# Weight sums made in DRAM: eleven of sixteen pairs of the joint down projection by seven products

## The chip, the cores and the metric

The kernel runs on one core of a Trainium2 chip. The metric is the device time of one execution in microseconds (us). The core has a matrix engine (PE, with its weight loads counted apart as PEld), a vector engine (DVE), a scalar engine (ACT) and GpSimd (POOL). SyncE (SP) issues most of the DMAs and POOL the others. A matmul takes a stationary operand from SBUF (128x128), streams a moving one (up to 512 columns) and adds into a bank of PSUM.

## The reference, cut to what matters

One block of a diffusion transformer with 256 tokens, 256 context tokens, a model width of 2048 and a feed-forward width of 5632, all in float32: adaptive layer norm, a projection to recurrent, attention and gate parts, a gated merge, and a convolutional feed-forward part. The change is in the last matmul of

```python
def conv_ffn(h, w_up, conv_w, conv_b, w_down):
    a, u = jnp.split(h @ w_up, 2, axis=-1)
    return (jax.nn.silu(depthwise_conv(a, conv_w, conv_b)) * u) @ w_down
...
        new_x = x_mid + mod_x[:, 5][:, None, :] * ffn_x
```

`w_down` is 5632 x 2048. Each column of `ffn_x` is scaled by a gate and added to `x_mid`.

## The kernel before, in words

**Precision.** Every float32 operand is split in two parts: `hi`, a cast by ACT, and `lo`, the rest, a subtraction by DVE. A product of two such operands is three matmuls (`mm3`): hi by hi, hi by lo and lo by hi. Below, "group" means such a three.

**The weight stream.** All weights lie in DRAM in one array `wst`, in rows of [128, 1024] floats (512 KB), in the order of use; SP fetches them. `Stream.load` and `chunk` do the same steps: load into a tile `raw` (five buffers), cast into `whi`, subtract into `wlo` (three buffers each). `chunk` keeps its casts and subtractions in the order of its calls. It can use a tile of its own instead: the tag `araw` has two buffers, which the `ada` loads use as well.

**Stages.** In order of time: norm statistics and the first adaptive parameters (0 to 150 us), the projections with the recurrent part and attention (to about 650 us), the gated merge (to about 790 us), the output projection (to about 917 us), the up projection in three groups of 16, 16 and 12 tiles of 128 feed-forward columns, and the down projection. After the first two up groups (about 917 to 1291 us) comes the joint stage, `down_two`: the down projection of their 32 tiles (1291 to 1456 us). Then come the third up group and its own down projection.

**The joint stage.** It has two halves, one for each 1024 output columns. A half walks 16 pairs of tiles. A pair is a product of 2x2 blocks: two token blocks by two feed-forward tiles, times two feed-forward tiles by two column blocks of 512. The function `half` makes it in one of two ways:

- A *plain* pair loads two rows (first `rb` with w21 and w22, then `ra` with w11 and w12) and makes eight groups, 24 matmuls.
- A *seven-product* pair (those in `SEVEN`) makes seven groups, 21 matmuls, from sums of blocks. The sums of activations (`s1`, `s2`, `s4`) are made by `seven_acts` when the up projection has made the two tiles. The four sums of weights, t1 to t4, are made by DVE within `half`: four adds of 128x512 in `four`, from `ra` and `rb` into two `araw` tiles, which are then split.

The splits of a seven-product pair are those of `rb` (two blocks), of w11 (one block, into a tile of its own, `wone`), of t1 and t3, and of t2 and t4. The groups follow in this order: two with w21 and w22, one with w11, two with t1 and t3, two with t2 and t4. The accumulators of the seven products are put together by `combine` after the last seven-product pair and by four more DVE operations at the half's end.

**Background work.** `ada_steps` makes the remaining adaptive parameters (`ada` below): 128 rows of 512 KB that POOL loads into `araw` and that DVE multiplies and adds into `acc`. The function `ada` advances it. It is called by hand in the early stages, by the stream according to `st.pace` (a call is due after 16/pace loads), and after each tile of the up projection (`up_evac`). `homes` tells in which buffers the loads land. The steps are given a lower priority than the work around them, by `LAG`.

**Residual rows.** `xn` holds the rows of `x_mid`, 2 MB in the tag `qo`, from the output projection to the end.

**Order of the work.** The kernel is written in the tile language. A planner orders each engine's instructions by priority, which is program order shifted by `high_priority`, when the tiles and data that they need are there in its plan. `issue_after` puts instructions behind a given one on the same engine.

Of the kernel before, what the change touches and what calls it, by code (L numbers as in the profile page):

```python
# [1 line left out]

# [5 lines left out]
F32 = mybir.dt.float32  # L8
F32R = mybir.dt.float32r
U32 = mybir.dt.uint32  # L10
AF = mybir.ActivationFunctionType
ALU = mybir.AluOpType
AX = mybir.AxisListType

P = 128
T = 256
D = 2048
KT = D // P
# [14 lines left out]
CONSTS = [("ident", 128), ("ones", 128), ("ropec", 256), ("ropes", 256), ("amask", 256), ("hmask", 256),  # L33
          ("m64", T)]
FF_GROUPS = [(0, 16), (16, 16), (32, 12)]
SEVEN = (1, 3, 5, 7, 9, 11, 13)
GSEVEN = (2, 4, 6)
LATE = (18, 20, 17)
LAST_ORDER = (1, 2, 4, 0, 3, 5)
# [15 lines left out]
def block_kernel(ctx, tc, xct, xr, prm, cst, ada2, wst, out):  # L55
    nc = tc.nc
    V, S, PE = nc.vector, nc.scalar, nc.tensor

    cons = ctx.enter_context(tc.tile_pool(name="cons", bufs=1))
    big = ctx.enter_context(tc.tile_pool(name="big", bufs=1))  # L60
# [5 lines left out]
    dram = ctx.enter_context(tc.tile_pool(name="dram", bufs=1, space=bass.MemoryType.DRAM))  # L66
# [36 lines left out]
    eps_c, one_c = par("eps"), par("one")  # L103
    S.preload_act_table_set("natural_log_exp_and_others")

    class Stream:
# [26 lines left out]
        def next(self, n=1):  # L133
            if self.pos == 8:
                self.load()
            sl = slice(self.pos * P, (self.pos + n) * P)
            self.pos += n
            return self.hi[:, sl], self.lo[:, sl]

    st = Stream()  # L140
# [3 lines left out]
    def chunk(parts, make, tag="raw", home=None):  # L144
        with tc.high_priority(offset=min(LEAD, max(0, tc.tile_snap_priority() - base[0]))), ExitStack() as inorder:
            raw = strm.tile([P, 1024], F32, name=tag, bufs=5 if tag == "raw" else 2) if isinstance(tag, str) else tag
            hi, lo = home or [strm.tile([P, 1024], F32R, name=nm, bufs=3) for nm in ("whi", "wlo")]
            for b in behind:
                inorder.enter_context(tc.issue_after(b.ins))
            make(raw)  # L150
            w = slice(0, 512 * parts)
            a = S.copy(hi[:, w], raw[:, w])  # L152
            b = V.tensor_tensor(lo[:, w], raw[:, w], hi[:, w].bitcast(F32), op=ALU.subtract)  # L153
            behind[:] = [a, b]
        return raw, [(hi[:, 512 * i:512 * i + 512], lo[:, 512 * i:512 * i + 512]) for i in range(parts)]

    def fetch(raw):
        nc.sync.dma_start(raw, wst[st.half])
        st.half += 1

    def split(hi, lo, src):
        S.copy(hi, src)
        V.tensor_tensor(lo, src, hi.bitcast(F32), op=ALU.subtract)

    def combine(sev, y, post):
        S.copy(y[0], sev[0])
        V.tensor_tensor(y[2], sev[2], y[0], op=ALU.subtract)
        V.tensor_tensor(y[1], sev[1], y[2], op=ALU.add)
        V.tensor_tensor(y[2], sev[3], y[2], op=ALU.add)
        V.tensor_tensor(y[3], sev[3], y[1], op=ALU.add)  # L170
        if post:
            for b in range(4):
                post(b)

    def half(act, order, seven, sums, banks, y, own, made={}, post=None, tail=False):

        norm, sev = banks

        def add(b, a, w, start=False, stop=False):
            mm3(b, *a, *w, start, stop)  # L180
        seven = [p for p in order if p in seven]
        plains = [p for p in order if p not in seven]
        for p in order:
            k1, k2 = 2 * p, 2 * p + 1
            rb, (w21, w22) = chunk(2, fetch)
            a11, a21, a12, a22 = act(k1, 0), act(k1, 1), act(k2, 0), act(k2, 1)
            st0, plain = p == order[0], p == plains[0]
            if p not in seven:
                if p == order[-1]:
                    ra, (w11, w12) = chunk(2, fetch)  # L190
                    for b, u1, u2, v1, v2 in ((0, a11, a12, w11, w21), (1, a11, a12, w12, w22), (2, a21, a22, w11, w21),
                                              (3, a21, a22, w12, w22)):
                        for w in [slice(0, 512)] if not tail or b < 3 else [slice(0, 256), slice(256, 512)]:
                            add(norm[b][:, w], u1, [v[:, w] for v in v1])
                            add(norm[b][:, w], u2, [v[:, w] for v in v2], stop=True)
                    break
                add(norm[0], a12, w21, st0)
                add(norm[2], a22, w21, st0)
                add(norm[1], a12, w22, st0)
                add(norm[3], a22, w22, plain)  # L200
                ra, (w11, w12) = chunk(2, fetch)
                add(norm[0], a11, w11)
                add(norm[2], a21, w11)
                add(norm[1], a11, w12)
                add(norm[3], a21, w12)
                continue
            f, l = p == seven[0], p == seven[-1]
            if f:
                sev = sev()
            s1, s2, s4, *s3 = sums[p]  # L210
            add(norm[0], a12, w21, st0)
            add(norm[1], s4, w22, st0)
            ra, (w11,) = chunk(1, fetch, home=own)
            add(sev[0], a11, w11, f, l)
            if p in made:
                t1, t3, t2, t4 = made[p]
                add(sev[1], s1, t1, f, l)
                add(sev[3], s3[0] if s3 else a21, t3, f, l)
                add(sev[2], s2, t2, f, l)
                add(norm[2], a22, t4, st0)  # L220
                if l:
                    combine(sev, y, post)
                continue

            r4 = strm.tile([P, 1024], F32, name="araw", bufs=2)

            def four(raw):
                V.tensor_tensor(raw[:, 0:512], ra[:, 0:512], ra[:, 512:], op=ALU.add)
                V.tensor_tensor(raw[:, 512:], ra[:, 512:], rb[:, 512:], op=ALU.add)  # L229
                V.tensor_tensor(r4[:, 0:512], raw[:, 0:512], rb[:, 512:], op=ALU.add)  # L230
                V.tensor_tensor(r4[:, 512:], r4[:, 0:512], rb[:, 0:512], op=ALU.add)
            r2, (t1, t3) = chunk(2, four, "araw")
            add(sev[1], s1, t1, f, l)
            add(sev[3], s3[0] if s3 else a21, t3, f, l)

            _, (t2, t4) = chunk(2, lambda raw: None, r4)
            add(sev[2], s2, t2, f, l)
            add(norm[2], a22, t4, st0)
            if l:
                combine(sev, y, post)  # L240
        if post:
            return
        with tc.high_priority(offset=RUSH):
            for b in range(4):
                V.tensor_tensor(y[b], norm[b], y[b], op=ALU.subtract if b == 2 else ALU.add)
# [218 lines left out]
    qo = big.tile([P, 2, H, T], F32, name="qo", tag="qo")  # L464
# [9 lines left out]
    homes = [wide]  # L474
# [38 lines left out]
                yield  # L513

    ada_it = ada_steps()

    def ada(n=1):
        with tc.high_priority(offset=-LAG), tc.issue_after(st.last.ins):
            for _ in range(n):
                next(ada_it, None)  # L520

    tasks = []

# [441 lines left out]
    for c in range(4):  # L965
        st.pace = 0
        if c % 2 == 0:
            norm = [bank() for _ in range(4)]
# [91 lines left out]
                norm2(2 * (k - 6))  # L1060


    def fold_pre(dst, o):
        b = smalltile(1)
        S.copy(b, o[:, T:T + 1])
        V.tensor_tensor(dst, o[:, 0:T], ssa[:, T:], op=ALU.mult)  # L1066
        S.activation(dst, dst, AF.Identity, bias=b)
# [31 lines left out]
    def seven_acts(p, gt, i, s1, s2):  # L1099
        if not sums:  # L1100
            sums["b"] = big.tile([P, 2, 2, 3 * P], F32R, name="sb", tag="sb")
        n = (SEVEN + LATE).index(p)
        if n == 2:
            sums["a"] = big.tile([P, 5, 2, 3 * P], F32R, name="sa", tag="v")
        d = sums["b"][:, n % 7] if n % 7 < 2 else spare2 if n > 7 else sums["a"][:, n - 2]
        sums[p] = d
        w = scr.tile([P, 512], F32, name="t")
        V.tensor_tensor(w[:, 0:P], s1[:, P:], s2[:, P:], op=ALU.subtract)
        s3 = w[:, 3 * P:] if p == LATE[-1] else s1[:, P:]
        V.tensor_tensor(s3, s1[:, P:], s1[:, 0:P], op=ALU.subtract)  # L1110
        V.tensor_tensor(w[:, P:2 * P], s1[:, 0:P], w[:, 0:P], op=ALU.subtract)
        V.tensor_tensor(w[:, 2 * P:3 * P], s2[:, 0:P], w[:, P:2 * P], op=ALU.subtract)
        if p == LATE[-1]:
            split(d[:, 0, :], d[:, 1, :], w)
            return
        split(gt[:, i - 1, 1, P:], gt[:, i - 1, 0, P:], s1[:, P:])
        split(d[:, 0, :], d[:, 1, :], w[:, 0:3 * P])
# [76 lines left out]
    up(1, g1)  # L1194
    for _ in ada_it:
        pass
    assert not tasks
    gate = [None, cst_t[:, 2 * P:2 * P + 1024]]
    line = to_line(gate2)
# [2 lines left out]
        get_rows(line, n, gate[n])  # L1202
    get_gate(1)
    y0, y1 = down_two(g0, g1)
    gate[0] = big.tile([P, 1024], F32, name="gate", tag="acc")
    get_gate(0)
    for b in range(4):
# [181 lines left out]
```

## Time and profile before

| | |
|---|---|
| median of three runs | 1658.97 us (1658.14 to 1659.23) |
| profiled execution | 1659.95 us |
| its span, first to last instruction | 1658.2 us |
| PE busy | 1640.0 us, 99% |
| DVE busy | 1303.4 us, 79% |
| ACT busy | 862.2 us, 52% |
| moved by DMA | 377.03 MB, 227 GB/s on average |

The profile is of one execution, and the time outside its span is launch and end. A row of a group gives the line of the kernel, the engine, the operation, the tiles written and read, the count, and then the busy time and the mean duration; behind the second bar stands the idle time of that engine just before these instructions and what ended it. A line such as L73 is that of a helper (all matmuls), so the tiles tell what is meant.

### The profile page before, as it was taken

How to read it: one execution, taken by the hardware profiler on the slowest of the kernel's cores; microseconds unless marked ns; L12 is line 12 of the kernel's file. 1: busy time of each engine (PE TensorE's matmuls, PEld its weight loads, DVE VectorE, ACT ScalarE, POOL GpSimd, SP SyncE). 2: the span in 40 equal slices, each digit the busy share in tenths (PEclk: the TensorE clock that was granted, in tenths of full speed). 3: DMA queues.
4: the chain of work that ended last, by engine and by line, in shares of the span. 5: the costliest groups of instructions: out<-in, count | busy, mean ns of one | idle time of the engine just before them, and what ended most of it. 6: DMA issues, size and time to landing. Idle time of an engine off the chain costs nothing.

```text
span 1658.2 us, 23679 instructions
## 1 busy us (share of the span) xinstructions
PE 1640.0 (99%) x8827; PEld 1356.2 (82%) x8827; DVE 1303.4 (79%) x2001; ACT 862.2 (52%) x1302; POOL 68.8 (4%) x133
## 2 busy tenths in 40 slices
PE   7999999999999999999999999999999999999998
PEld 3668888888888888888888988888888888888887
DVE  3448986675889976888888798878877898998788
ACT  4336553443645664545445665555555555556552
POOL 0000100100000000000011000000000000000000
PEclk9999999999999999999999999999999999999999
DMA  9996834634456665676878577767655566666654
GB/s 379 407 373 242 298 117 153 204 110 151 166 204 206 219 216 174 239 278 213 314 258 312 171 239 263 251 224 267 238 190 189 202 206 201 217 208 223 218 189 165
DMA packets 104260, 377.03 MB, mean 227 GB/s; under 512 B 11696, under 2 KB 12112, under 8 KB 103888
## 3 DMA queue, kind: packets, MB, share of 16 engines
q1 hardware_dynamic: 85568, 307.87, 52.2%
q0 software_dynamic: 18576, 67.64, 12.6%
q8 instruction: 69, 1.13, 0.3%
q14 instruction: 47, 0.39, 0.1%
HBM read 373.36 MB, written 2.11 MB: 226 GB/s over the span
## 4 chain that ended last, share of the span: by engine, by line
PE 87%; DVE 5%; DMA 4%; issue 3%; ACT 1%; SPq 0%; POOL 0%; DVEq 0%; ACTq 0%; POOLq 0%
PE bankm L73 76%; PE banks L73 9%; DMA ringv<-in_wst_dram 1%; DVE wlo L119 1%; DMA ringq<-in_wst_dram 1%; DVE acc L497 1%; DMA ringkT<-in_wst_dram 1%; PE banks L505 0%; PE banks L872 0%; DMA araw<-in_ada_dram 0%; DMA xraw<-in_xct_dram 0%; PE banks L705 0%; PE banks L900 0%; PE banks L697 0%; ACT whi L118 0%
## 5 line engine op out<-in xcount | busy, mean ns | idle before, releaser
L73 PE MATMUL bankm<-hl,whi 128*128 128x512 f32 (+1 forms) x2048 | 626.6, 388 | 0.1
L118 ACT CAST whi<-raw 128x1024 fp32r<-128x1024 f32 (+1 forms) x378 | 394.4, 1045 | 390.4 <-PE bankm L73 339.6
L119 DVE TENSOR_TENSOR wlo<-raw,whi 128x1024 fp32r<-128x1024 f32 (+1 forms) x378 | 459.0, 1216 | 175.6 <-ACT whi L118 174.5
L73 PE MATMUL bankm<-whi,hl 128*128 128x512 f32 x1548 | 498.1, 393 | 1.2 <-ACT hl L340 0.9
L73 PE MATMUL bankm<-hl,wlo 128*128 128x256 f32 (+2 forms) x1760 | 396.0, 293 | 1.3 <-DVE wlo L119 1.3
L73 PEld LDWEIGHTS bankm<-hl,wlo 128*128 128x128 f32 x1760 | 330.5, 188 | 75.9 <-DVE wlo L119 2.2
L73 PEld LDWEIGHTS bankm<-hl,whi 128*128 128x128 f32 x2048 | 327.6, 189 | 17.6 <-DVE fs L1066 0.4
L73 PEld LDWEIGHTS bankm<-whi,hl 128*128 128x128 f32 x1548 | 289.6, 188 | 63.2 <-ACT hl L340 2.6
L73 PE MATMUL bankm<-wlo,hl 128*128 128x512 f32 x774 | 301.6, 390 | 0.0
L73 PEld LDWEIGHTS bankm<-wlo,hl 128*128 128x128 f32 x774 | 145.4, 188 | 29.1 <-DVE wlo L119 0.2
L497 DVE SCALAR_TENSOR_TENSOR acc<-araw,csil,acc 128x1024 f32<-128x1024 f32 x120 | 153.2, 1277 | 0.7 <-DMA araw<-in_ada_dram 0.2
L153 DVE TENSOR_TENSOR wlo<-raw,whi 128x1024 fp32r<-128x1024 f32 x95 | 115.7, 1223 | 30.3 <-ACT whi L152 26.7
L152 ACT CAST whi<-raw 128x1024 fp32r<-128x1024 f32 x95 | 99.9, 1054 | 73.3 <-PE bankm L73 53.1
L492 POOL DMA_DIRECT2D araw<-in_ada_dram x128 | 68.1, 532 | 1111.9 <-DVE acc L497 635.3
L73 PE MATMUL bankm<-whi,yb 128*128 128x512 f32 x256 | 82.1, 396 | 0.0
L152 ACT CAST whi<-araw 128x1024 fp32r<-128x1024 f32 x44 | 46.2, 1053 | 62.5 <-DVE araw L229 56.2
L73 PEld LDWEIGHTS bankm<-whi,yb 128*128 128x128 f32 x256 | 47.9, 188 | 10.0
L153 DVE TENSOR_TENSOR wlo<-araw,whi 128x1024 fp32r<-128x1024 f32 x44 | 53.7, 1222 | 1.8 <-ACT whi L152 0.5
L73 PE MATMUL bankm<-wlo,yb 128*128 128x512 f32 x128 | 50.4, 394 | 0.0
L1079 ACT ACTIVATE fs<-fs,prm 128x256 f32<-128x256 f32 x44 | 26.4, 601 | 45.7 <-DVE fs L554 45.7
L73 PE MATMUL bankm<-whi,g 128*128 128x512 f32 x124 | 41.3, 389 | 0.0
L321 DVE TENSOR_REDUCE tn<-banks 128x8 f32<-128x32 f32 (+1 forms) x9 | 1.7, 187 | 45.9 <-ACT whi L118 42.8
(346 smaller groups left out, 1704.0 us busy)
## 6 DMA issues: line engine op xcount, KB each, us to landing
raw<-in_wst_dram SPq DMA_DIRECT2D x495, 512.0 KB, 4.1
araw<-in_ada_dram POOLq DMA_DIRECT2D x128, 512.0 KB, 4.7
ringv<-in_wst_dram SPq DMA_DIRECT2D x24, 512.0 KB, 10.1
ringq<-in_wst_dram SPq DMA_DIRECT2D x20, 512.0 KB, 9.9
araw<-in_wst_dram SPq DMA_DIRECT2D x10, 512.0 KB, 9.9
xraw<-in_xct_dram SPq DMA_DIRECT2D x8, 512.0 KB, 8.3
raw<-in_wst_dram SPq DMA_DIRECT2D x7, 384.0 KB, 9.9
ringkT<-in_wst_dram SPq DMA_DIRECT2D x5, 512.0 KB, 9.9
```

The costliest lines, as they stand in the source:

```text
L73: return PE.matmul(o, l, r, start=start, stop=stop, skip_group_check=True)
L118: S.copy(hi, raw)
L119: self.last = V.tensor_tensor(lo, raw, hi.bitcast(F32), op=ALU.subtract)
L152: a = S.copy(hi[:, w], raw[:, w])
L153: b = V.tensor_tensor(lo[:, w], raw[:, w], hi[:, w].bitcast(F32), op=ALU.subtract)
L321: V.tensor_reduce(m8, aps[:, 0:w].rearrange("p (q g c) -> p q c g", q=2 * n, g=4)[:, :, 0:2, :], axis=AX.X, op=ALU.add)
L492: nc.gpsimd.dma_start(raw, ada2[idx])
L497: V.scalar_tensor_tensor(acc, raw, csil[:, kt, 0:1], acc, op0=ALU.mult, op1=ALU.add)
L1079: S.activation(t, s, AF.Identity, bias=cb[:, f:f + 1], scale=cw[:, f, 1:2])
```

## The change

- `SEVEN` grows from seven to eleven of the sixteen pairs: 1, 2, 3, 5, 6, 7, 9, 10, 11, 13, 14. Pairs 0, 4, 8, 12 and 15 remain plain.
- For each half and each of these pairs a DRAM tile `d` of [128, 2, 1024] floats is filled by POOL: one copy of the pair's two rows, and four transfers of [128, 512] that add into their destination. At the end it holds t4, t2 and t1, t3. These are 22 copies and 88 adding transfers.
- They are issued by `ada`: two steps per call, or one where `st.pace` is set, and none while `homes` is `apart` or `late`. Ahead of them DVE writes one element (`pins`) and POOL copies it, so that POOL waits for DVE to come to that place.
- In `half` such a pair loads the first half of `ra` only (w11) and takes t1, t3 and t4, t2 by two SP loads into `araw`. The adds by DVE are not used in the joint stage any more.
- The sums of activations of four more pairs need room, and take it in the tag `qo`. `xn` leaves it: it is written to a DRAM tile `kept` by POOL after the norm of the up projection, and read back into a new tile in `qo` after the joint stage in program order.

```diff
-SEVEN = (1, 3, 5, 7, 9, 11, 13)
+SEVEN = (1, 2, 3, 5, 6, 7, 9, 10, 11, 13, 14)
...
+    def fetch_half(raw):
+        nc.sync.dma_start(raw[:, 0:512], wst[st.half, :, 0:512])
+        st.half += 1
+
+    dsums = {}
+    JOINT = wst.shape[0] - 24 - 2 * FF_GROUPS[2][1] * KT // 8 - 64
+
+    def sum_steps(n):
+        ds = []
+        for p in SEVEN:
+            at = JOINT + 32 * n
+            d = dram.tile([P, 2, 1024], F32, name="sum%d" % len(dsums))
+            dsums[at, p] = d
+            ds.append((d, at + 2 * p))
+        for d, r in ds:
+            yield lambda d=d, r=r: nc.gpsimd.dma_start(d, wst[r:r + 2].rearrange("k p c -> p k c"))
+        for d, r in ds:
+            yield lambda d=d, r=r: nc.gpsimd.dma_start(d[:, 1, 0:512], wst[r + 1, :, 512:], accum_op=ALU.add)
+        for d, r in ds:
+            yield lambda d=d, r=r: nc.gpsimd.dma_start(d[:, 1, 512:], wst[r, :, 512:], accum_op=ALU.add)
+        for d, r in ds:
+            yield lambda d=d, r=r: nc.gpsimd.dma_start(d[:, 0, 512:], d[:, 1, 0:512], accum_op=ALU.add)
+        for d, r in ds:
+            yield lambda d=d, r=r: nc.gpsimd.dma_start(d[:, 0, 0:512], d[:, 0, 512:], accum_op=ALU.add)
+
+    sum_it = itertools.chain(sum_steps(0), sum_steps(1))
...
-            ra, (w11,) = chunk(1, fetch, home=own)
+            ra, (w11,) = chunk(1, fetch_half if (at, p) in dsums else fetch, home=own)
...
+            if (at, p) in dsums:
+                d = dsums[at, p]
+                _, (t1, t3) = chunk(2, lambda raw: nc.sync.dma_start(raw, d[:, 1]), "araw")
+                add(sev[1], s1, t1, f, l)
+                add(sev[3], s3[0] if s3 else a21, t3, f, l)
+                _, (t4, t2) = chunk(2, lambda raw: nc.sync.dma_start(raw, d[:, 0]), "araw")
...
             for _ in range(n):
                 next(ada_it, None)
+            fs = list(itertools.islice(sum_it, 0 if homes[0] in (apart, late) else 1 if st.pace else 2))
+            if fs:
+                pin = pins[:, len(pinned) % 40:len(pinned) % 40 + 1]
+                V.tensor_copy(pin, one_c)
+                pinned.append(nc.gpsimd.tensor_copy(pin, pin))
+                with tc.issue_after(pinned[-1].ins):
+                    for f in fs:
+                        f()
...
+    kept = dram.tile([P, 2, 2, 1024], F32, name="kept")
+    nc.gpsimd.dma_start(kept, xn)
...
+        if n == 2:
+            sums["c"] = big.tile([P, 5, 2, 3 * P], F32R, name="sc", tag="qo")
+        if n == 6:
             sums["a"] = big.tile([P, 5, 2, 3 * P], F32R, name="sa", tag="v")
...
     y0, y1 = down_two(g0, g1)
+    xn = big.tile([P, 2, 2, 1024], F32, name="xn", tag="qo")
+    nc.gpsimd.dma_start(xn, kept)
```

More of the change, by code (lines that the diff above doesn't have):

```diff
@@ L1 @@
+import itertools
 from contextlib import ExitStack
@@ L177, in half @@
         norm, sev = banks
+        at = st.half
         def add(b, a, w, start=False, stop=False):
@@ L218, in half @@
                 add(sev[3], s3[0] if s3 else a21, t3, f, l)
+                add(sev[2], s2, t2, f, l)
+                add(norm[2], a22, t4, st0)
+                if l:
+                    combine(sev, y, post)
+                continue
+            if (at, p) in dsums:
[4 more added lines that the diff above has]
+                _, (t4, t2) = chunk(2, lambda raw: nc.sync.dma_start(raw, d[:, 0]), "araw")
                 add(sev[2], s2, t2, f, l)
@@ L515, in block_kernel @@
     ada_it = ada_steps()
+    pins = cons.tile([P, 40], F32, name="pins")
+    pinned = []
     def ada(n=1):
@@ L1102, in seven_acts @@
         n = (SEVEN + LATE).index(p)
+        m = len(SEVEN)
         if n == 2:
+            sums["c"] = big.tile([P, 5, 2, 3 * P], F32R, name="sc", tag="qo")
+        if n == 6:
             sums["a"] = big.tile([P, 5, 2, 3 * P], F32R, name="sa", tag="v")
-        d = sums["b"][:, n % 7] if n % 7 < 2 else spare2 if n > 7 else sums["a"][:, n - 2]
+        d = sums["b"][:, n % m] if n % m < 2 else spare2 if n > m else sums["c"][:, n - 2] if n < 6 else sums["a"][:, n - 6]
         sums[p] = d
@@ L1196, in block_kernel @@
         pass
+    assert next(sum_it, None) is None
     assert not tasks
```

## The prediction

> **What bounds the kernel now.** I began with the page: busy time, slices, queues.
>
> ```profile
> span 1658.2 us, 23679 instructions
> PE 1640.0 (99%) x8827; PEld 1356.2 (82%) x8827; DVE 1303.4 (79%) x2001; ACT 862.2 (52%) x1302; POOL 68.8 (4%) x133
> PEclk9999999999999999999999999999999999999999
> q1 hardware_dynamic: 85568, 307.87, 52.2%
> q0 software_dynamic: 18576, 67.64, 12.6%
> ```
>
> PE is never short of clock and is busy 99% of the span, so a change pays only through fewer products, or costs through new waits of PE. The joint stage (first matmul at 1291 us, last at 1456) and the stages that get new work I then read in the table of windows.
>
> ```profile
> 150.00:206.00 56.00, 54.72 (x358) 46.66 (x357) 55.02 (x89) 32.79 (x57) 8.46 (x16) 1.00 0.81 285
> 206.00:290.00 84.00, 83.75 (x596) 70.13 (x595) 63.29 (x144) 36.49 (x76) 4.19 (x8) 1.00 0.41 138
> 290.00:446.00 156.00, 156.00 (x914) 129.71 (x913) 108.48 (x215) 69.22 (x130) 9.58 (x19) 1.00 0.45 152
> 446.00:490.00 44.00, 43.43 (x270) 35.40 (x269) 38.80 (x76) 23.30 (x44) 3.18 (x6) 1.00 0.59 205
> 490.00:650.00 160.00, 159.95 (x753) 131.31 (x752) 130.08 (x226) 90.66 (x142) 8.47 (x16) 1.00 0.63 211
> 956.00:1291.00 335.00, 335.00 (x1931) 292.40 (x1930) 264.41 (x389) 188.46 (x294) 14.82 (x28) 1.00 0.67 232
> 1291.00:1374.00 83.00, 82.75 (x365) 67.58 (x364) 73.67 (x86) 45.77 (x52) 0.00 (x0) 1.00 0.61 209
> 1374.00:1456.00 82.00, 82.00 (x364) 67.83 (x363) 74.84 (x86) 44.98 (x47) 0.00 (x0) 1.00 0.64 209
> ```
>
> The columns are busy PE, weight loads, DVE, ACT and POOL, then clock, DMA share and GB/s. In both halves of the joint stage PE idles 0.25 us in 165; DVE is at 90%, the DMA engines at 61 to 64%. One window is different: from 150 to 206 us DVE is full (55.02 of 56) and the DMA share is 0.81. The chain of waits gives the pace of a plain pair and a seven-product pair of the joint stage:
>
> ```profile
> 1322.36 8.16 PE bankm L73 x36
> 1330.52 2.04 PE banks L73 x9
> ```
>
> 45 products take 10.20 us, 0.2267 us each. A plain pair (24) takes 5.44 us, a seven-product pair (21) takes 4.76.
>
> **The change, part by part.**
>
> *Removed products.* Four more pairs in each half, 8 in all, lose 3 products each: 24 x 0.2267 = **-5.4 us**, all of it on the path, since PE does not wait. This is the whole prize, 0.33%.
>
> *Removed sums on DVE.* 14 pairs (before) lose four adds of 128x512 each:
>
> ```profile
> L228 DVE TENSOR_TENSOR araw<-raw 128x512 f32<-128x512 f32 x13 | 8.9, 685 | 0.0
> L153 DVE TENSOR_TENSOR wlo<-araw,whi 128x1024 fp32r<-128x1024 f32 x27 | 33.0, 1222 | 0.8
> L152 ACT CAST whi<-raw 128x1024 fp32r<-128x1024 f32 x45 | 47.3, 1054 | 25.1 <-PE bankm L73 16.4 <-PE banks L73 8.7
> ```
>
> That is 56 x 0.685 = 38 us of DVE, hidden behind PE before, so worth nothing by itself.
>
> *New loads in the joint stage.* A seven-product pair now loads 0.524 MB (second row) + 0.262 (half of the first) + 2 x 0.524 (the sums) = 1.835 MB; it loaded 1.049. Over 22 such pairs and 10 plain ones that is 50.9 MB; at PE's pace (726 - 24 products, 159 us) it is 320 GB/s, and by the window rows (0.61 at 209 GB/s) a share of 0.93. It still fits; the point is the buffers. Both sums go to tile "araw", which has two buffers, one for each sum of a pair. So a sum's buffer must be loaded, cast by ACT, subtracted by DVE and freed once per pair. The hops, from the timeline:
>
> ```profile
> 1328.44 2.51 DVE L153 TENSOR_TENSOR wlo<-araw,whi 128x1024 fp32r<-128x1024 f32 x2
> 1331.01 1.23 DVE L153 TENSOR_TENSOR wlo<-raw,whi 128x1024 fp32r<-128x1024 f32 x1
> 1331.92 1.05 ACT L152 CAST whi<-raw 128x1024 fp32r<-128x1024 f32 x1 [0.94 <-PE banks L73]
> 1332.26 6.82 SPq L158 DMA_DIRECT2D raw<-in_wst_dram  x4
> 1333.00 2.59 DVE L153 TENSOR_TENSOR wlo<-raw,whi 128x1024 fp32r<-128x1024 f32 x2 [0.77 <-ACT whi L152]
> ```
>
> DVE ends at 1332.24 and SP issues at 1332.26; ACT ends at 1332.97 and DVE starts at 1333.00. With 0.03 from landing to ACT, the circle is L + 0.03 + 1.05 + 0.03 + 1.22 + 0.02 = L + 2.35 us, L being the time from issue to landing of 512 KB. It has to be no longer than 4.76 us, so L no longer than 2.41. The first line below is that of "raw" from 1300 to 1445 us, the second that of 750 to 900 us, where 282 GB/s moved:
>
> ```profile
> DMA to landing us min/median/max: 3.0/3.5/5.7
> raw<-in_wst_dram SPq DMA_DIRECT2D x54, 512.0 KB, 4.8
> ```
>
> No landing there is as short as 2.41. At 320 GB/s I take **3.65 us**: the joint stage's own row, raised a little, since a sum's load is issued when its buffer frees and not from a long queue. Bounds 3.0 and 4.8. So each seven-product pair that follows another one comes 6.00 - 4.76 = 1.24 us late, against what the first of a group has in hand. That is: the split tiles whi and wlo have three buffers and a seven-product pair uses all three, so the split of its last sum cannot begin before the plain pair ahead of it is done; it takes 0.03 + 1.05 + 0.03 + 1.22 = 2.33 us, and PE needs it after five groups of three products and one product, 3.63 us: 1.30 us in hand. The groups are (1,2,3), (5,6,7), (9,10,11), (13,14). A group of three stalls 2 x 1.24 - 1.30 = 1.18 us, a group of two not at all (0.06 left). Pair 15 is last and plain, and each of its groups needs its second row: two splits behind that of pair 14 (2.51 us, the first of these lines) against 1.13 us of products left and 0.23: 1.15 - 0.06 = 1.1 us. One half: 3 x 1.18 + 1.1 = 4.6; both: **+9.3 us**. At L = 3.0 it is 0.9, at 3.5 it is 7.2, at 4.8 (1.09 for the group of two, too) it is 25.
>
> By the Trainium skill ("DMA: Bandwidth & Descriptors", section "Anatomy of one DMA — SWDGE (gpsimd) path") a transfer costs about 2.0 us and its bytes at 436 GB/s, an estimate of 3.2 us for 512 KB; the stalls would be 3.4 us and the sum 1662. The row's median, 3.5, is longer at two thirds of the traffic, so I stay with the row.
>
> *Making the sums.* 22 copies of 1.049 MB and 88 adding transfers of 0.262 MB go through POOL's queue, 2 steps per `ada` call (1 where `st.pace` is set). Counting the calls: 30 before the attention part (60 steps), 30 up to 650 us (30 steps), none while homes are `apart` or `late`, the last 20 after 956 us. No row shows a DRAM-to-DRAM copy or an add. The nearest is the same queue from 150 to 206 us, and the issues there:
>
> ```profile
> q0 software_dynamic: 2144, 7.83, 41.8%
> araw<-in_ada_dram POOLq DMA_DIRECT2D x16, 512.0 KB, 4.8
> DVE acc L495 <- DMA araw<-in_ada_dram: 2.7, 1, 2.7
> ```
>
> 0.418 x 56 us for 7.83 MB is 2.99 us of all 16 engines per MB: 69 us for the copies and 69 for the adds, twice that if an add counts both things it reads. From 150 to 650 us fall 122 to 176 of these; the windows have 223 free (the sum of each one's length by one minus its share). Overall it fits; between 150 and 206 it does not. 16 `ada` loads mean about 10 calls, so 11 copies and 9 adds, 41 us or more where 11 are free. They spill to 206 to 290, where 50 are free, but `ada` loads stand behind them in POOL's queue, and `acc` on a full DVE waits for those; splits and PE stand behind `acc`. Bounds: 0 (`acc` is simply done later) and 30 us (all that spills is on the path). I take 2.5, near the lower end, because the ordering is free to put `acc` later and because the copies need not be done early. The 70 pins are tiny DVE copies; the nearest op is
>
> ```profile
> L508 DVE TENSOR_TENSOR modv<-modv,prm 128x8 f32<-128x8 f32 x2 | 0.3, 155 | 0.0
> ```
>
> 0.155 us: 10 in the full window, 1.5 us; elsewhere DVE has room. POOL's wait on a pin holds up only POOL's later loads and sums. Together **+4 us**.
>
> *More activation sums.* Four pairs more go through `seven_acts` in the up stage:
>
> ```profile
> L1108 DVE TENSOR_TENSOR t<-fs 128x128 f32<-128x128 f32 x4 | 1.1, 284 | 0.0
> L163 DVE TENSOR_TENSOR sa<-t,sa 128x384 fp32r<-128x384 f32 x4 | 2.2, 556 | 1.1 <-ACT sa L162 1.1
> ```
>
> 4 x 0.285 + 0.556 + about 0.14 for one split cut in two: 1.84 us a pair, 7.4 in all, in a window with 71 us of free DVE and PE at 335.00 of 335. **0**; without that cover 7.4.
>
> *Rows parked.* xn goes out (2.1 MB, 6.3 us at 2.99) with 0.33 of 335 us of DMA free: 0. It comes back through POOL when the sums in "qo" are last used, pair 7 of the second half, beside loads at a share of 0.93. Bounds 0 and 6.3; I take **+1**, since eight pairs (some 40 us) remain before it is needed and the plain ones have spare DMA.
>
> **Sum.** -5.4 + 9.3 + 4 + 1 = +8.9 on the profiled execution's 1659.95 (1.75 of it outside the span): 1668.8. That execution lies 0.98 above the median, so **1668** against 1658.97.
>
> **Rivals.**
>
> *The circle does not bind* (faster). If the loads land in 3.0, the shortest row, and the sums cost nothing: 0.9 - 5.4 = -4.5, **1654.4**. For it: the two loads of a pair are only two in a short queue. Against: the median is 3.5 at less traffic. From L = 3.3 upward it is no longer faster by a measurable amount. Chance 0.27.
>
> *Between the two*: L near 3.4 and sums for 0 to 2 us: 1656 to 1662. Chance 0.14.
>
> *DMA latency under load.* L = 4.8: -5.4 + 25 + 4 + 1 = +25, **1683**. For it: the row of 750 to 900 us, at less traffic than 320 GB/s. Against: there POOL loaded too, and SP fetched far ahead. Chance 0.14. The Trainium skill says in the same page ("Latency and other measured facts") that an HBM access takes 0.2 us on average and 2 us at high load; the two rows, 3.5 and 4.8, point the same way.
>
> *Making the sums hits the path.* `acc` waits behind copies from 150 to 206: half of the 30 us in place of 4: **1679**. For it: the one row in which DVE already waited for an `ada` load. Against: DVE would have to keep its order. Chance 0.12.
>
> That the sums aren't used is excluded: both sides take the row number from the same count.
>
> **How the numbers follow.** The forecast itself, 1662 to 1674, has 0.33. My bound for a change is 0.2%, 3.3 us, about what can be told apart here. Faster: 0.26, from the first rival. Same: 0.15. Slower: 0.59. The range for 8 in 10 runs from the first rival, **1654**, to the third, **1684**; the forecast's own is 1662 to 1674.
>
> **What would show it.** Right: PE idle of 8 to 10 us in the joint stage, its ACT casts of "araw" preceded by waits for DMA, most in pairs 3, 7, 11 and 15; SP waiting for DVE's subtract on "araw"; products in the stage down from 726 to 702. Wrong: a joint stage of 160 us; landings at 3.0; PE gaps from 150 to 290 us instead, with DVE waiting for `araw<-in_ada_dram`. Loads at 4.8 or more would make 1668 too low.

## The result, and the profile after

The changed kernel takes **1708.43 us** (median of four, 1705.45 to 1709.03) against 1659.1 beside it: a ratio of **1.0294**, 95% interval 1.0276 to 1.0312. It is slower, as forecast, but by 49 us in place of 9, far outside the range of 1654 to 1684. The profiled execution took 1705.45 us, the shortest of the four; what the others spent besides, no trace shows. The page of the kernel after, busy time, clock and queues:

```profile
span 1703.5 us, 24033 instructions
PE 1655.0 (97%) x8803; PEld 1353.6 (79%) x8803; DVE 1291.5 (76%) x2055; ACT 876.2 (51%) x1326; POOL 194.3 (11%) x315
PEclk9999979999999999999999999999999999999999
q0 software_dynamic: 37520, 117.98, 24.8%
```

The 24 products are gone, yet PE idles 48.5 us where it idled 18.2, and the row of the clock has a dent in one slice (213 to 256 us). Where the 45.3 us of span went is seen from the chains of waits, that is, from the work that ended last, followed back to what released it. First two stretches of the chain of before, then the chain of after, in which the same two stretches (40 and 256 products) come back:

```profile
225.98 9.09 PE bankm L73 x40
...
1246.66 44.60 PE bankm L73 x256
```

```profile
174.25 22.22 DMA sum<-in_wst_dram
196.75 19.81 DMA araw<-in_ada_dram
...
244.25 9.09 PE bankm L74 x40
...
1264.95 44.59 PE bankm L74 x256
```

The offset is 18.27 us by 244 us and still 18.29 at 1265: the whole **early loss** lies before 244 us, and nothing is lost in the thousand microseconds after it. The joint stage then runs from 1309.3 to 1502.3, 193.0 us, where it took 165.9: **+27.0**. What comes behind it takes 201.2 us in both. 18.3 + 27.0 = 45.3.

The windows of after, with the columns of the prediction's table (the short ones show the places where the clock fell):

```profile
150.00:206.00 56.00, 55.47 (x358) 46.36 (x358) 44.42 (x88) 31.62 (x55) 16.87 (x25) 1.00 0.97 378
206.00:290.00 84.00, 70.97 (x504) 57.06 (x504) 67.15 (x149) 32.55 (x68) 28.88 (x43) 0.88 0.91 262
224.00:230.00 6.00, 5.44 (x45) 3.12 (x48) 4.63 (x17) 1.37 (x3) 5.21 (x7) 0.50 1.07 322
232.00:234.00 2.00, 2.00 (x6) 1.61 (x5) 1.52 (x3) 0.28 (x1) 0.53 (x1) 0.50 1.14 207
234.00:236.00 2.00, 2.00 (x10) 1.57 (x10) 1.57 (x5) 0.07 (x1) 0.74 (x1) 0.97 1.12 240
490.00:650.00 160.00, 160.00 (x747) 131.56 (x746) 137.65 (x268) 90.86 (x145) 38.16 (x64) 1.00 0.90 273
956.00:1291.00 335.00, 334.90 (x1970) 294.16 (x1969) 273.12 (x428) 193.59 (x310) 33.80 (x58) 1.00 0.77 253
1309.00:1405.00 96.00, 87.82 (x359) 66.48 (x358) 63.49 (x66) 51.91 (x61) 0.00 (x0) 0.98 0.80 271
1329.00:1333.00 4.00, 3.48 (x9) 2.48 (x9) 3.37 (x3) 2.80 (x3) 0.00 (x0) 0.60 0.60 216
1405.00:1508.00 103.00, 92.84 (x385) 70.74 (x385) 68.50 (x71) 53.34 (x59) 0.53 (x1) 0.97 0.81 276
1469.00:1473.00 4.00, 3.80 (x9) 3.02 (x10) 3.11 (x4) 1.77 (x4) 0.00 (x0) 0.50 0.64 210
```

From 150 to 206 us the DMA engines are full (0.97, before 0.81), and DVE, which was full (55.02 of 56), now waits (44.42). From 490 to 650 they are nearly as full (0.90) and PE loses nothing: here a full DMA was dear only where something near the path waited for a transfer. The timeline shows what did, POOL's issue of an `ada` load, then DVE and PE (in brackets the idle time before, and what ended it):

```profile
196.75 0.53 POOL L533 DMA_DIRECT2D araw<-in_ada_dram  x1 [3.98 <-DMA sum<-in_wst_dram]
...
208.48 1.29 DVE L538 SCALAR_TENSOR_TENSOR acc<-araw,csil,acc 128x1024 f32<-128x1024 f32 x1 [11.60 <-DMA araw<-in_ada_dram]
...
224.56 0.43 PE L74 MATMUL banks<-hb 128*32 128x64 f32 x4 [13.03 <-DVE hb L699]
```

For one `ada` load DVE waits 11.60 us, until 208.48. A later one, on the chain above, is late twice: POOL issues it at 196.75, when the copy issued at 174.25 has landed after 22.22 us, and it then takes 19.81 us to land itself. The recurrent part's operations on `hb` come behind these `acc` operations on DVE, the last at 224.22, and PE stands 13.03 us for them. When it goes on, the granted clock is 0.50 until 234 us, so of these 9.5 us about 4.8 are lost besides. 13.0 + 4.8 = 17.8 of the early loss of 18.3.

In the joint stage, one full turn of an `araw` buffer, from SP's issue to SP's next issue into it:

```profile
1339.20 0.33 SPq L256 DMA_DIRECT2D araw<-sum  x1
...
1344.07 1.05 ACT L153 CAST whi<-araw 128x1024 fp32r<-128x1024 f32 x1 [1.55 <-DMA araw<-sum]
1345.15 1.23 DVE L154 TENSOR_TENSOR wlo<-araw,whi 128x1024 fp32r<-128x1024 f32 x1 [1.29 <-ACT whi L153]
1346.40 0.33 SPq L256 DMA_DIRECT2D araw<-sum  x1
```

7.20 us against the 4.76 that PE needs for a pair: the landing (from issue until the data are there) takes 4.87 of it, the hops 2.33. Over the whole stage the landings of "araw" are

```profile
DMA to landing us min/median/max: 3.5/4.9/9.9
```

and the table of waits of after has both losses (total, times, longest):

```profile
ACT whi L153 <- DMA araw<-sum: 48.0, 26, 4.4
...
DVE acc L538 <- DMA araw<-in_ada_dram: 18.2, 5, 11.6
```

The longest wait of the joint stage stands beside the parked rows. In program order the read stands behind the stage, but POOL issues it while the second half still runs, and a sum's load that SP issues 4.6 us later has the longest landing of the stage, 9.9 us:

```profile
1452.32 0.53 POOL L1264 DMA_DIRECT2D xn<-kept  x1 [247.28 <-ACT whi L153]
...
1456.90 0.33 SPq L256 DMA_DIRECT2D araw<-sum  x1
...
1466.85 1.04 ACT L153 CAST whi<-araw 128x1024 fp32r<-128x1024 f32 x1 [4.40 <-DMA araw<-sum]
...
1467.94 0.79 PE L74 MATMUL bankm<-whi,sa 128*128 128x512 f32 x1 [3.90 <-ACT whi L153]
```

Behind these 3.90 us the clock is half until 1473, some 2.6 us more. The same is seen in the four other kernels in which both sums of a pair share a tag (e1, e6, e7 and e11 below): there, too, the longest wait of PE in the stage, 3.7 to 4.6 us, ends 13 to 16 us behind the read's issue. That the read makes it is inferred; no run takes the read out of these kernels.

### The profile page after: what moved, and what is told of

Read it like the earlier page. It is cut to its first block, busy times and chain, and to the rows that moved or that the text cites. A ratio compares the mean times of both kernels' runs of the same rounds, so it can differ in the third digit from the quotient of the medians.

```text
span 1703.5 us, 24033 instructions
## 1 busy us (share of the span) xinstructions
PE 1655.0 (97%) x8803; PEld 1353.6 (79%) x8803; DVE 1291.5 (76%) x2055; ACT 876.2 (51%) x1326; POOL 194.3 (11%) x315
## 3 DMA queue, kind: packets, MB, share of 16 engines
q0 software_dynamic: 37520, 117.98, 24.8%
## 4 chain that ended last, share of the span: by engine, by line
PE 80%; DMA 10%; DVE 5%; issue 3%; ACT 2%; POOL 0%; SPq 0%; ACTq 0%; DVEq 0%; POOLq 0%
PE bankm L74 71%; PE banks L74 7%; DMA araw<-sum 4%; DMA araw<-in_ada_dram 2%; ACT whi L153 1%; DVE wlo L154 1%; DMA sum<-in_wst_dram 1%; DMA ringv<-in_wst_dram 1%; DMA ringq<-in_wst_dram 1%; DVE wlo L120 1%; DMA ringkT<-in_wst_dram 1%; DVE acc L538 1%; PE banks L923 0%; PE banks L546 0%; PE banks L756 0%
## 5 line engine op out<-in xcount | busy, mean ns | idle before, releaser
L74 PE MATMUL bankm<-whi,hl 128*128 128x512 f32 x1524 | 491.5, 393 | 1.6 <-ACT hl L381 1.0
L74 PEld LDWEIGHTS bankm<-whi,hl 128*128 128x128 f32 x1524 | 285.4, 188 | 63.7 <-ACT hl L381 2.6
L74 PE MATMUL bankm<-wlo,hl 128*128 128x512 f32 x762 | 297.0, 391 | 0.0
L533 POOL DMA_DIRECT2D araw<-in_ada_dram x128 | 77.6, 630 | 818.5 <-DVE acc L538 359.0
L538 DVE SCALAR_TENSOR_TENSOR acc<-araw,csil,acc 128x1024 f32<-128x1024 f32 x120 | 153.2, 1277 | 18.6 <-DMA araw<-in_ada_dram 18.2
L154 DVE TENSOR_TENSOR wlo<-raw,whi 128x1024 fp32r<-128x1024 f32 x87 | 105.5, 1221 | 23.2 <-ACT whi L153 21.0
L153 ACT CAST whi<-raw 128x1024 fp32r<-128x1024 f32 x87 | 90.8, 1052 | 60.4 <-PE bankm L74 46.0
L154 DVE TENSOR_TENSOR wlo<-araw,whi 128x1024 fp32r<-128x1024 f32 x60 | 73.4, 1224 | 58.7 <-ACT whi L153 58.1
L153 ACT CAST whi<-araw 128x1024 fp32r<-128x1024 f32 x60 | 63.1, 1051 | 91.7 <-DMA araw<-sum 48.0
L568 POOL COPY pins<-pins 128x1 f32<-128x1 f32 x70 | 41.8, 598 | 133.0 <-DVE pins L567 132.9
L358 ACT COPY t<-banks 128x512 f32<-128x512 f32 (+1 forms) x9 | 4.9, 541 | 62.6 <-PE banks L74 62.6
```

The source lines that it names most:

```text
L74: return PE.matmul(o, l, r, start=start, stop=stop, skip_group_check=True)
L358: S.copy(rows[:, 0:w], aps[:, 0:w])
L533: nc.gpsimd.dma_start(raw, ada2[idx])
L538: V.scalar_tensor_tensor(acc, raw, csil[:, kt, 0:1], acc, op0=ALU.mult, op1=ALU.add)
L568: pinned.append(nc.gpsimd.tensor_copy(pin, pin))
```

## The experiments

There were rival theories for each loss; the expectations give them. The early loss is what is lost ahead of the joint stage. Early: the copies and adds make `ada` loads late, and DVE and PE with them, or something else does it, such as weights that come late. Where it is the `ada` loads, their order in POOL's queue may be the cause, or the engines being full. Joint: the circle of the two `araw` buffers, whose cure is buffers, or simply too many bytes, whose cure would be none.

One reading in the expectations has to be put right first. Several speak of a wait of about 5 us at the end of the joint stage, which came from taking the next stage's first product as the end. There is no such wait. The timeline of PE in e3_late_and_two_tags:

```profile
1454.44 0.49 PE L74 MATMUL bankm<-hl,whi 128*128 128x512 f32 x1
1454.77 0.39 PE L74 MATMUL bankm<-wlo,g 128*128 128x512 f32 x1
...
1459.35 0.39 PE L74 MATMUL bankm<-hl,whi 128*128 128x512 f32 x1
```

One product of the third up group (`hl,whi`) runs ahead of the last 4.6 us of the joint stage (`g`, pair 15), without idle time. The stage ends at 1459.35. In the table the joint stage is counted to the true end; figures in the expectations that end at the early product are 4.8 to 5.2 us shorter wherever pair 14 is made by seven products, and the 200 us in that of e2 run past the end. Each ratio is to executions of the kernel before taken beside that run, with medians of 1658.6 to 1659.2. The last two columns are of one profiled execution each; that of e8 was the shortest of eleven (1656.79).

| kernel | median, us | ratio (95%) | joint stage starts | joint stage, us |
|---|---|---|---|---|
| before | 1659.1 | | 1291.0 | 165.9 |
| after | 1708.43 | 1.0294 (1.0276 to 1.0312) | 1309.3 | 193.0 |
| e1_late_sums | 1690.17 | 1.0186 (1.0171 to 1.0202) | 1289.3 | 197.8 |
| e2_sums_two_tags | 1682.31 | 1.0144 (1.0127 to 1.0161) | 1311.0 | 168.5 |
| e3_late_and_two_tags | 1664.33 | 1.0037 (1.0024 to 1.0050) | 1290.4 | 169.0 |
| e4_sums_unused | 1679.96 | 1.0121 (1.0106 to 1.0136) | 1309.0 | 167.5 |
| e5_last_pair_earlier | 1662.08 | 1.0016 (1.0007 to 1.0025) | 1289.8 | 168.9 |
| e6_copies_by_act | 1720.86 | 1.0372 (1.0358 to 1.0386) | 1320.8 | 195.6 |
| e7_sums_in_raw_tag | 1674.20 | 1.0088 (1.0074 to 1.0102) | 1288.6 | 182.0 |
| e8_last_pair_earlier_and_rows_in_two | 1659.85 | 1.0004 (0.9995 to 1.0013) | 1289.1 | 164.6 |
| e9_ten_pairs | 1659.57 | 1.0002 (0.9993 to 1.0010) | 1290.7 | 165.1 |
| e10_nine_pairs | 1655.80 | 0.9979 (0.9970 to 0.9988) | 1289.0 | 163.0 |
| e11_sums_first | 1705.24 | 1.0275 (1.0261 to 1.0289) | 1304.3 | 197.2 |

**No sums in the first twelve calls of `ada`.**

```diff
+    calls = [0]
...
+            calls[0] += 1
-            fs = list(itertools.islice(sum_it, 0 if homes[0] in (apart, late) else 1 if st.pace else 2))
+            fs = list(itertools.islice(sum_it, 0 if calls[0] <= 12 or homes[0] in (apart, late) else 1 if st.pace else 2))
```

> The changed kernel, but the first 12 calls of the background step issue no sums, so the first eleven copies fall some 60 us later, where DVE and the DMA engines have room. Theory 1 (the copies stood ahead of the ada loads in POOL's queue while DVE was full, and DVE waited in order): the 18.2 us lost before 300 us are gone, the joint stage stays as it is, 1690 us. Theory 2 (the traffic of the sums costs its time wherever it lies): the loss moves to a later stage and the time stays near 1708.

1690.17, as the first theory said. The early windows of e1:

```profile
150.00:206.00 56.00, 56.00 (x367) 48.16 (x366) 55.10 (x90) 33.34 (x59) 8.11 (x16) 1.00 0.83 292
206.00:290.00 84.00, 83.73 (x596) 70.14 (x595) 63.76 (x148) 36.62 (x76) 13.32 (x24) 1.00 0.64 235
```

PE idles 0.27 us in 140 (1.53 before the change), at full clock, and the joint stage starts 20.0 us earlier than in after. So it is the sums at that place that make the early loss. The joint stage keeps its loss (197.8; its clock is 0.98 and 0.95).

**One of the two sums of a pair in the five buffers of "raw".**

```diff
-                _, (t1, t3) = chunk(2, lambda raw: nc.sync.dma_start(raw, d[:, 1]), "araw")
+                _, (t1, t3) = chunk(2, lambda raw: nc.sync.dma_start(raw, d[:, 1]), "raw")
```

> The changed kernel, but the first of a pair's two sum loads goes to the tag of the weight rows (five buffers) and only the second to araw, so an araw buffer has two pairs' time for its circle instead of one. Same bytes, same splits, same products. Theory 1 (the circle load, cast, subtract, free of about 7.25 us per pair sets the joint stage): the joint stage falls from 200 us to 160 to 166, the total to 1670 to 1677. Theory 2 (the DMA engines or DRAM are the limit: 50.9 MB at the 275 GB/s seen there): no less than 185 us there, total 1693 or more.

1682.31, above the 1670 to 1677 that were expected, and the joint stage is 168.5 us where it was 193.0. The bytes are the same, so it was the circle and not the bytes. Not all came back: 702 products at 0.2267 are 159.1 us, with the 1.3 that the stage of before has over its products 160.4, so 8 us of waits stay.

**Both edits.**

> Both edits together. Theory 1: the two losses are separate and both go: 1652 to 1660, about the kernel before. Theory 2: 1677 or more.

1664.33, above the 1652 to 1660 that were expected. But the gains of e1 and e2 are 18.3 and 26.1, 44.4 together, and both edits give 44.1: the losses are two and independent. The joint windows of e3, then its landings in "araw":

```profile
1290.00:1372.00 82.00, 80.32 (x349) 64.48 (x348) 61.96 (x63) 51.63 (x60) 0.00 (x0) 1.00 0.87 304
1372.00:1454.00 82.00, 78.83 (x340) 62.91 (x338) 60.05 (x59) 50.48 (x55) 0.58 (x1) 1.00 0.91 324
```

```profile
DMA to landing us min/median/max: 4.0/5.9/11.0
```

More moves per microsecond than in after, each load into "araw" lands later (a median of 5.9 for 4.9), and yet PE stalls less: "araw" now takes one load per pair, so its two buffers leave 2 x 4.76 - 2.35 = 7.2 us for a landing where they left 2.41.

**Sums made, and not read.** `sum_steps` keeps the eleven pairs; the joint stage has its seven old pairs with the sums by DVE.

```diff
-SEVEN = (1, 2, 3, 5, 6, 7, 9, 10, 11, 13, 14)
+SUMMED = (1, 2, 3, 5, 6, 7, 9, 10, 11, 13, 14)
+SEVEN = (1, 3, 5, 7, 9, 11, 13)
...
-            if (at, p) in dsums:
+            if False:
```

> All copies, adds and the parked rows are made as in the changed kernel, but the joint stage is that of before (seven pairs, sums by DVE); the sums in DRAM are not read. Theory 1 (two separate losses): only the early one, 1659 + 18 = 1677. If the parked rows or the later adds cost something too, it shows here above 1677; if the early loss needs the new joint stage, 1659.

1679.96, above the first theory's 1677, which left open a price of the rows. The joint stage starts at 1309.0, 18.0 late, and takes 167.5, 1.6 more than before. So making the sums and parking the rows has a price of its own of about 20 us.

**Pair 14 exchanged for pair 12, on top of both edits.**

```diff
-SEVEN = (1, 2, 3, 5, 6, 7, 9, 10, 11, 13, 14)
+SEVEN = (1, 2, 3, 5, 6, 7, 9, 10, 11, 12, 13)
```

> Late sums and two tags as in e3, and the eleventh seven-product pair is 12 instead of 14, so the last one (13) has two plain pairs behind it, as in the kernel before. In e3 PE waits 4.4 us when the up projection begins again after the joint stage. Theory 1 (the accumulators of the seven products are put together only after pair 14, and the next stage wants their banks one pair later): that wait goes, 1659 to 1661. Theory 2 (the wait comes from the parked rows that are read back): it stays, 1664.

1662.08, between the two theories. The joint stage is 168.9 us, e3's is 169.0: the exchange did nothing there in the profiled executions, and the wait that it was to remove did not exist. The medians of e3 and e5, taken at different times, differ by 2.2 us with ranges that overlap (1662.74 to 1667.67, 1658.99 to 1664.46); what makes this difference stays open.

**The copies issued from ACT's queue**, so that POOL's `ada` loads don't stand behind them (the adds stay with POOL).

```diff
-                S.copy(hi, raw)
+                self.cast = S.copy(hi, raw)
...
-            yield lambda d=d, r=r: nc.gpsimd.dma_start(d, wst[r:r + 2].rearrange("k p c -> p k c"))
+            def copy(d=d, r=r):
+                with tc.issue_after(st.cast.ins):
+                    nc.scalar.dma_start(d, wst[r:r + 2].rearrange("k p c -> p k c"))
+            yield copy
```

> The changed kernel, but the 22 copies are issued on ACT's DMA queue behind the cast of the current weight row, not on POOL's; the adds stay on POOL's. Same bytes at about the same time. Theory 1 (ada loads stood behind copies in POOL's own queue): most of the 18 us before 300 us goes, 1690 to 1694. Theory 2 (the sixteen DMA engines are full from 150 to 230 us, whichever queue the copies are in): the loss stays at 12 to 18 us, 1702 to 1708.

1720.86, slower still and above both theories. The table of waits of e6 from 150 to 300 us, then POOL's issues ahead of one load:

```profile
DVE acc L541 <- DMA araw<-in_ada_dram: 19.4, 4, 14.0
...
PE banks L74 <- DVE hb L699: 17.9, 1, 17.9
```

```profile
196.72 1.71 POOL L182 DMA_DIRECT2D sum<-in_wst_dram  x2
...
198.45 1.76 POOL L182 DMA_DIRECT2D sum<-in_wst_dram  x2
199.56 1.76 POOL L536 DMA_DIRECT2D araw<-in_ada_dram  x2
```

The joint stage starts 11.5 us later than in after. With the copies out of POOL's queue, an `ada` load issued at 200.71 still took 29.2 us to land, so a copy ahead of it in that queue isn't needed to make it late. The DMA engines were full (a share of 0.93 from 150 to 206 us, 1.04 from 200 to 230), and that is the likelier cause. But four adding transfers were issued in POOL's queue within the 4 us ahead of this load, so the queue's part in it isn't excluded; no run takes the adds out of it too.

**Both sums in "raw", sums late** (a dose between e1 and e3): e1, and "raw" for "araw" in both loads.

> As e1 (late sums), but both sum loads go to the weight rows' tag of five buffers, which then takes four tiles per seven-product pair: 1.25 pairs or 5.95 us for the circle of load, cast, subtract and free, between the one pair (4.76) of e1 and the 1.7 to 2 pairs of e3. Theory 1 (the circle): a joint stage between the 193 us of e1 and the 164 us of e3, about 172 by a circle of 7.25 us (1.3 us late per pair that follows another), total 1669 to 1674. Theory 2 (araw is special, not the number of buffers): 164 us, as e3, total 1664.

1674.20, at the upper end of what was expected. The joint stage is 182.0: between 197.8 and 169.0, as the circle wants it, but 10 longer than the 172 that were expected. Its casts wait 34.8 us for the sums' loads, in 30 places.

A pair now makes four loads into five buffers: by the same estimate as above a landing may take 5/4 x 4.76 - 2.35 = 3.6 us. In e3 it is 5/3 x 4.76 - 2.35 = 5.6 for "raw", less than the 5.9 measured in "araw" beside it; that e3's remaining waits come from this is an inference from the estimate.

**The parked rows read back in two halves**, the second held back until DVE has reached the results of the stage's first half; on top of e5.

```diff
-    nc.gpsimd.dma_start(xn, kept)
+    nc.gpsimd.dma_start(xn[:, :, 1], kept[:, :, 1])
+    pin = pins[:, 39:40]
+    with tc.issue_after(st.last.ins):
+        V.tensor_copy(pin, y1[0][:, 0:1])
+    pinned.append(nc.gpsimd.tensor_copy(pin, pin))
+    with tc.issue_after(pinned[-1].ins):
+        nc.gpsimd.dma_start(xn[:, :, 0], kept[:, :, 0])
```

> As e5, and the parked rows come back in two loads of 1 MB, the second only after the joint stage. In e3 PE loses about 4 us in the second half just behind the 2 MB read. Theory 1 (that read delays the weight loads): 2 us less than e5, 1657 to 1659. Theory 2 (it does not): as e5.

1659.85, 2.2 us less than e5 beside it (0.8 to 3.7 by the spread of eleven executions each): reading the 2 MB at once cost about that much. The gain of four pairs more in each half is now just eaten by what waits remain.

**Ten and nine pairs.** e8 with one pair and with two pairs fewer per half; in the second no more than two stand in a row.

```diff
-SEVEN = (1, 2, 3, 5, 6, 7, 9, 10, 11, 12, 13)
+SEVEN = (1, 2, 3, 5, 6, 7, 9, 10, 12, 13)
```

> As e8, with ten seven-product pairs (1, 2, 3, 5, 6, 7, 9, 10, 12, 13): groups of three, three, two and two, 6 pairs more than before in both halves, 4.1 us of products less. Theory (what is left of the loss in e8 comes where several seven-product pairs follow each other, five in its last group): fewer stalls by 2 to 3 us against 1.4 us of products given back, 1657 to 1659, a little below the kernel before. If the stalls that are left have nothing to do with the length of the groups: 1661.

```diff
-SEVEN = (1, 2, 3, 5, 6, 7, 9, 10, 11, 12, 13)
+SEVEN = (1, 2, 4, 5, 7, 8, 10, 11, 13)
```

> As e8, with nine seven-product pairs in groups of two (1, 2, 4, 5, 7, 8, 10, 11, 13): 4 pairs more than before in both halves, 2.7 us of products less. Same theory: almost no stalls in the joint stage, 1656.5 to 1658.5. If not: 1662.

Ten pairs: 1659.57, above the 1657 to 1659 that were expected and no different from before. Nine pairs: **1655.80** (expected 1656.5 to 1658.5), a ratio of 0.9979, the one version that beats the kernel before. Windows of its joint stage, and its loads there (KB each, median us to landing):

```profile
1288.00:1370.00 82.00, 82.00 (x364) 67.56 (x363) 61.40 (x63) 49.19 (x57) 0.00 (x0) 1.00 0.86 299
1370.00:1454.00 84.00, 83.75 (x372) 69.03 (x371) 64.42 (x67) 50.19 (x53) 1.95 (x3) 1.00 0.86 299
```

```profile
araw<-sum SPq DMA_DIRECT2D x16, 512.0 KB, 5.6
```

PE idles 0.25 us: with no more than two seven-product pairs in a row the waits are gone, though each load lands later than in after. 12 products fewer than before at 0.2267 are 2.7 us, the stage is 2.9 shorter, the median 3.4. Nine such pairs pay more than eleven. Whether it is their number or the plain pair behind every two, this run can't tell, since both changed.

**The sums first, the `ada` steps after**: in the first twelve calls sums are issued and no `ada` step; those owed are made up one per call later.

```diff
+    calls, owed = [0], [0]
...
+            calls[0] += 1
+            owed[0] += n
+            n = 0 if calls[0] <= 12 else min(owed[0], n + 1)
+            owed[0] -= n
```

> The changed kernel, but the first 12 calls of the background step issue their sums and no ada load; the ada steps left out are caught up one per call afterwards. So the same copies meet the same weight loads from 150 to 230 us, without ada loads behind them. Theory 1 (DVE waits in order for ada loads that land late, and PE for DVE): the early loss falls to 4 us or less, 1690 to 1695. Theory 2 (the copies slow SP's weight loads enough to starve PE): it stays near 18, 1705 to 1710.

1705.24: by its number it misses the first theory, which wanted an early loss of at most 4 and 1690 to 1695; the loss was 13.3, and 1705.24 lies within the second theory's 1705 to 1710 (with a joint stage 4.2 us longer than in after). The windows tell the two theories apart better than the total does. The windows of e11, and its first wait for an `ada` load:

```profile
150.00:206.00 56.00, 56.00 (x366) 48.34 (x365) 40.08 (x87) 34.43 (x58) 17.42 (x30) 1.00 1.02 359
206.00:290.00 84.00, 78.49 (x561) 65.72 (x560) 57.96 (x135) 33.78 (x70) 17.53 (x27) 0.96 0.73 201
```

```profile
DVE acc L536 <- DMA araw<-in_ada_dram: 8.2, 1, 8.2
```

While the sums ran alone the engines were full (1.02) and PE lost nothing in 56 us, so it is not the weights that starve. The loss begins when `ada` loads come back: the first was on the chain for 11.27 us, DVE stood 8.2 us for it, and PE 4.9 us for DVE. That agrees with the mechanism, at another place. By the chains the offset to before is 4.1 us at 284 us and 9.8 at 385. The step between is the same wait once more, where the owed steps are made up:

```profile
352.17 1.28 DVE L538 SCALAR_TENSOR_TENSOR acc<-araw,csil,acc 128x1024 f32<-128x1024 f32 x1 [4.45 <-DMA araw<-in_ada_dram]
...
356.92 0.49 PE L74 MATMUL banks<-hb 128*128 128x128 f32 x2 [3.15 <-DVE hb L763]
```

The clock is 0.72 from 356 to 362 us. The last 3.5 of the 13.3 us come behind 385 us and aren't traced here.

## Why the prediction went wrong, step by step

*What bounds the kernel; removed products.* Right. PE's pace of 0.2267 holds where it doesn't wait and the clock is full: e10's 714 products are 161.9 us, and its stage takes 163.0.

*New loads, the circle.* The mechanism was right to 0.02 us: the hops after landing were put at 2.35 and measured 2.33, and two tags in place of one took 24.5 us of the stage away (e2). The term mis-sized is the landing L, put at 3.65 and measured **4.9**. At 4.9 the prediction's own formula gives 2.49 late per pair, 3.68 for a group of three, 1.19 for a group of two and 1.15 at the end, 26.8 for both halves in place of 9.3. The step that failed is the choice of the row: a median of 4.8 at 282 GB/s stood there, and it was set aside because "POOL loaded too, and SP fetched far ahead". After the change SP loads nearly alone in the stage, moves 271 to 276 GB/s, and the loads land in 4.9: the reason for setting the row aside did not hold. The estimate of 3.2 from the Trainium skill ("DMA: Bandwidth & Descriptors", section "Anatomy of one DMA — SWDGE (gpsimd) path") was further off; that section is about transfers issued by GpSimd, and these were SP's. The median measured under this load, 4.9, decides. (At 3.2 the prediction's formula gives stalls of 3.0 us, not 3.4; the sum of 1662 stays.)

*The clock.* It was not in the prediction, which took PE's pace as given. The half clock cost about 4.8 us of the early loss, and in the joint stage 1.7 (0.60 from 1329 to 1333 us) and 2.6 (until 1473). The joint stage's loss over its products is 27.0 + 5.4 = 32.4 us. The idle time in its windows, 18.3 us, is less, because each product is shown as busy for 0.39 us though they follow each other every 0.2267. Counted from the start of a product to the start of the next, 24.4 us are lost at the 29 waits that the timeline lists and 8.4 elsewhere (the half clock, and waits too short to be listed; the kernel before has 0.8 us of both together). About 6.5 of this stand beside the parked rows and 1.7 are the other fall of the clock, so the circle's own part is some 25 us, near the formula's 26.8. The division is an estimate: a load that came late beside the rows might have been late without them.

*Making the sums.* The mechanism was named (copies fill 150 to 206 us, `acc` waits for its load, splits and PE stand behind `acc`), and its place was right. The value was wrong: 2.5 (and 1.5 for the pins) taken from bounds of 0 and 30, measured 18.3. The reason given, that "the ordering is free to put `acc` later", failed: DVE stood at `acc` for 11.6 us with `hb` behind it. The engine time was low too. Queue q0 took 24.8% of 1703.5 less 12.6% of 1658.2, 213 us, for 50.3 MB more (sums and parked rows): 4.2 us per MB in place of 2.99, if the `ada` loads took what they took before. It lies near the upper bound of "twice that if an add counts both things".

*Pins, activation sums, rows.* The up stage hid the activation sums as said: 334.90 of 335. Parking the rows was put at 1 and cost 1.6 (e4) to 2.2 (e8 against e5) where few of the joint stage's loads were late otherwise. In the kernel after, where most of the sums' loads were late already, the wait beside the read and the half clock behind it are about 6.5 us; that the read is their cause is inferred.

*The rivals.* Both unfavourable ones came true at once, and so did two of the signs that the prediction named for being wrong: DVE waiting for `araw<-in_ada_dram`, and landings of 4.8 or more. They were priced as alternatives, 1683 and 1679, though nothing made them exclude each other. Together, with their own terms, they give -5.4 + 25 + 15 + 1 = +35.6, about 1695; the losses of clock, 9.1 us, make it 1704, and the profiled execution took 1705.45. That this comes so near is partly luck: the 15 was half of a bound, and the wait was 13.0. Such a sum should have been a case of its own and the upper end of the range.

## What to carry to other kernels

A tile's buffers allow a landing of (buffers / loads per step) x step - processing; set this against landings measured at the traffic that the change itself will cause, not at the traffic before it. Background transfers cost PE 18 us here where loads that DVE waits for in order shared the full DMA engines, and nothing at a share of 0.90 elsewhere: read each window's DMA share and who waits for what before placing them. If a gain is paid for in waits, try less of it: nine pairs gained where eleven lost.

## What the runs showed of the hardware that was not expected

From the page of after, issues of transfers (KB each, median us to landing):

```profile
sum<-in_wst_dram POOLq DMA_DIRECT2D x22, 1024.0 KB, 11.9
...
sum<-in_wst_dram POOLq DMA_DIRECT2D x44, 256.0 KB, 9.1
sum<-sum POOLq DMA_DIRECT2D x44, 256.0 KB, 8.1
```

An adding transfer of 256 KB took 8 to 9 us to land in the median, where SP's plain loads of 512 KB from the same DRAM tiles took 4.9, later and beside other traffic. Copies, adds and parked rows together held the 16 engines for 4.2 us per MB, by the difference worked out above.

In the kernel after, the clock fell at the longest waits of PE only. In the early place PE stops at 211.5 us; the clock is half from about 214 us, and PE's next product, at 224.56, is followed by 9.5 us at half clock. In the joint stage the timeline lists 29 waits of PE, and the clock falls in two places, at the waits of 1.51 us (ended at 1328.81) and 3.90 us (ended at 1467.94); the other waits, of at most 1.02 us, leave it at 1.00. Behind the 3.90 us it takes 5 us to come back. Length alone doesn't decide: in e6 a wait of 1.70 us (ended at 178.62) left the clock at 1.00. The Trainium skill says ("TensorE: Matmul & The Clock Gate", section "What's actually happening") that the idle state is half the clock, and that it ends after at least one busy stretch of about 3.4 us. The trace agrees on the half; the way back, 5 and 9.5 us, was longer than one such stretch, which the "at least" allows.

POOL's copy of a single element per partition, the second half of each pin, is not small:

```profile
L568 POOL COPY pins<-pins 128x1 f32<-128x1 f32 x70 | 41.8, 598 | 133.0 <-DVE pins L567 132.9
```

0.6 us each by the trace, where DVE's nearest small op took 0.155.
